# Sixteen on-chip transposes per attention head moved from TensorE to VectorE block turns with a trip through memory, with small edits at the start and the end

## The chip, the cores and the metric

One NeuronCore of one Trainium2 chip runs the whole program; nothing is shared with other cores. The metric is the device time of one execution in microseconds (us). TensorE (PE in the profile) does matrix products and transposes into PSUM, VectorE (DVE) and ScalarE (ACT) do elementwise work, GpSimd (POOL) does some more of it and issues a few DMAs, and SyncE (SP) issues nearly all DMAs, in order.

## The reference, cut to what matters

A two-layer decoder trunk on 1024 positions of width 1024, all in float32: first a gated linear recurrence (RG-LRU), then forgetting attention with 16 heads of 64, and a final RMS norm. The change is mostly in the attention:

```python
logits = einsum("bqhd,bkhd->bhqk", q_blk, kf) * scale
logits = logits + (cq_blk[..., :, None] - ck[:, :, None, :])   # cum: running sum of log sigmoid(f)
logits = where(kpos[None, :] <= qpos[:, None], logits, NEG_INF)
p = softmax(logits, axis=-1)
o = einsum("bhqk,bkhd->bqhd", p, vf)          # then y = o * silu(gate); y @ w_out
```

The mask is causal. The 1024 queries are 8 blocks of 128 rows, i = 0 to 7, and the keys 8 blocks of 128, j = 0 to 7; block i needs keys up to block i.

## The kernel before, in words

Every product is done in three float32r matmuls, high times high, high times low and low times high, so each operand is split into a high part (a cast, `to_hi`, mostly on ACT) and a low part (a subtraction, `to_lo`, mostly on DVE or POOL). Layer 0 takes the first 460 us or so of the span. Layer 1 then goes through 16 heads, two to a pair; while a head's attention runs, PE also computes the projections of the next pair (`kq_units`, `g_units`, `values`), which are called the fill here. One step of fill is six matmuls of 512 columns.

For one head hd there are four generators, and two calls of `run` interleave them by a string: a digit takes the next step of that generator, a dot takes one step of fill.

- `maxima(hd, c)` (L698) works on query blocks i = 4c to 4c+3. For each block PE computes the logits S (a PSUM tile of tag "S" with 1024 columns), DVE applies the mask and takes the row maximum in place (L715, "mask" below), and ACT writes the exponentials p to SBUF with their row sums (L720). These p have a query on each partition.
- `weigh(hd, c)` (L751) needs p with a key on each partition. For a pair of key blocks, PE transposes 128x128 pieces of p into a PSUM tile `pt`, also of tag "S" (L58); ACT and DVE split it into ph and pl (L85, L96); one step later PE adds V times ph and V times pl to the output O. The half c = 0 has the key pairs (0,1) and (2,3); the half c = 1 has (0,1), (2,3), (4,5) and (6,7). For c = 1 the pairs (0,1) and (2,3) are full: eight transposes each.

The first `run` of a head has `weigh(hd, 0)` as 0 and `maxima(hd, 1)` as 1, the second has `weigh(hd, 1)` as 0 and `maxima(hd + 1, 0)` as 1. The order strings are

```python
ORDER = "1.0.1.1.1.0.0", "10.1.0.1.01.0.0"              # heads 0 to 11
LAST = "1..0.1..1..1.0.0", "10..1.0..1.01..0..0"        # heads 12 to 15
```

PSUM tag "S" has two buffers, so a new S or pt has to wait until the last but one has been read by everybody. The instruction order of each engine within these rules is fixed when the program is built, by a planner that estimates times. Each engine then runs its own list strictly in order and waits on semaphores. SP's list too is in order: an issue that waits holds back all issues behind it. It holds the weight loads (`wf`), the loads of each head's K and Q parts (T, U; `load` and `load_q`) and the stores of finished heads (`y1d`).

At the start, SP loads a first piece of weights, then x in 16 pieces of 128x512 with the rest of the first weights in between; ACT squares each piece and makes its high part, DVE sums squares and makes the low part (`split_x`, `square_x`). At the end, `turned` makes the last rows, `root_mean` their norm, and SP stores them.

Of the kernel before, what the change touches and what calls it, by code (L numbers as in the profile page):

```python
# [11 lines left out]
F32 = mybir.dt.float32  # L12
# [26 lines left out]
def trunk(ctx: ExitStack, tc: tile.TileContext, xt, w0, wg, wo0, pc, gn, gf, w1, wv, wf, bf, wo1, out):  # L39
# [26 lines left out]
    epst = const.tile([P, 1], F32, name="epst")  # L66
    nc.vector.memset(epst, EPS)
    root = const.tile([P, 1], F32, name="root")
    nc.scalar.activation(root, epst, AF.Sqrt)
# [6 lines left out]
    pct = const.tile([P, 8, NB], F32, name="pct")  # L76
    gnt = const.tile([P, 2, KT], F32, name="gnt")
    cw = [pct[:, j] for j in range(4)]
# [26 lines left out]

    def split_weights(src, shape, hi_eng, lo_eng, parts=wpool):
        wt = loaded(shape)
        for part, sl in src:
            nc.sync.dma_start(wt[:, :, sl], part)
# [73 lines left out]
    with ExitStack() as l0:  # L183
# [41 lines left out]
        first = ([], [])  # L225
        early = [weights(w0[0], lo_eng=nc.vector), weights(w0[NB], lo_eng=nc.gpsimd)]
        k = 0
        for step in "uxnxgxuxgxxpxxxxxxxxxx":
            if step == "n":
                nc.sync.dma_start(gnt, gn)  # L230
            elif step == "p":
# [10 lines left out]
        def split_x(h, layer=0):  # L242
            for k, (hi, lo) in enumerate((raw, hT)[layer][h]):
                g_ = gnt[:, layer, k : k + 1]
                x = xs[h][k]
                to_hi(hi, x, nc.scalar, scale=g_)
                nc.vector.scalar_tensor_tensor(lo, x, g_, f32(hi), ALU.mult, ALU.subtract)
                yield
# [4 lines left out]
        def square_x(h):  # L253
            to = acc[:, halves[h]]
            sums[h].append(to)
            for k in range(KT):
                z = sq[k % 4] if k else to
                nc.scalar.activation(z, xs[h][k], AF.Square)
                if k == KT - 1:
                    sums[h].append(z)  # L260
                elif k:
                    nc.vector.tensor_tensor(to, to, z, ALU.add)
                yield
# [12 lines left out]

        for _ in zip(split_x(0), square_x(0)):
            pass

# [110 lines left out]
        for n in range(NB):  # L390
# [8 lines left out]
            if n == 0:  # L399
                gps = held[0] = two_banks("gps")  # L400
                product(gps[:, 0], 0, first[1])
                for _ in zip(split_x(1), square_x(1)):
                    pass
                done = norm_row(0)
            else:
# [86 lines left out]
    with ExitStack() as l1:  # L492
# [139 lines left out]
        def forget(half):  # L632
            cs = slice(half * HALF, (half + 1) * HALF)
            pt = ps.tile([P, HALF], F32, tag="O", name="fps")
            for i in range(4):
                if half and i > 1:
                    yield
                with tc.issue_after(pe[0].ins):
                    transpose(pt[:HEADS, i * P : (i + 1) * P], fz[:, half * 4 + i], ident)
            z_, e_ = (at.tile([HEADS, HALF], F32, tag=t, name=n, bufs=3) for t, n in (("ph", "z"), ("pl", "e")))  # L640
            parts = [at.tile([HEADS, HALF], F32R, tag=f"p{i + 2 * half}", name="cp", bufs=1) for i in (3, 4)]
            hi, lo = parts
# [47 lines left out]
        stats, ps_ = {}, {}  # L690

        def maxima(hd, c):

            s = hd % 2
            pair = hd // 2
            if c == 0:
                stats[hd] = at.tile([P, 8], F32, tag="sums", name="sums")
            sums = stats[hd]  # L698
            for i in range(4 * c, 4 * c + 4):
                n = (i + 1) * P  # L700

# [16 lines left out]

                p = ps_[i] = at.tile([P, n], F32, tag=f"p{i}", name="p", bufs=1)
                seen[0] = nc.scalar.activation(  # L720
                    p, S[:, :n], AF.Exp, bias=m, scale=-1.0, accum_out=sums[:, i : i + 1]
                )
# [26 lines left out]
        def weigh(hd, c, sub=slice(0, HALF)):  # L749
# [7 lines left out]
            O = ps.tile([P, HALF], F32, tag="O", name="O")[:, : end - begin]  # L757
            nj = end // P
            def products(j0, qlo, parts):
                for j, q, (ph, pl) in zip((j0, j0 + 1), qlo, parts):  # L760
                    v = V[j][:, 2 * s : 2 * s + 2].rearrange("p a d -> p (a d)")
                    o = O[:, q - begin :]
                    matmul(o, v, ph, start=j == 0, stop=False)
                    matmul(o, v, pl, start=False, stop=j == nj - 1)

            held = None
            for j0 in range(0, nj, 2):
                A = ps.tile([P, 2, HALF], F32, tag="S", name="pt")
                qlo = [max(begin, j * P) for j in (j0, j0 + 1)]
                ns = [end - q for q in qlo]  # L770
                for jj in range(2):
                    ks = slice((j0 + jj) * P, (j0 + jj + 1) * P)
                    for q in range(qlo[jj], end, P):
                        o = q - qlo[jj]
                        transpose(A[:, jj, o : o + P], ps_[q // P][:, ks], ident)
                parts = []
                for jj in range(2):
                    a = A[:, jj, : ns[jj]]
                    ph, pl = (at.tile([P, HALF], F32R, tag=t, name=t, bufs=3)[:, : ns[jj]] for t in ("ph", "pl"))
                    to_hi(ph, a, nc.scalar)  # L780
                    parts.append((ph, pl))
                for jj, (ph, pl) in enumerate(parts):
                    to_lo(pl, A[:, jj, : ns[jj]], ph, nc.vector)
                if held:
# [113 lines left out]
        def turned(c, q):  # L898
# [7 lines left out]
            elif q == 0:  # L906
                res = [tu.tile([P, SEQ], F32, tag=t, name="res") for t in ("U", "U0")]
            else:
                res = [tu.tile([P, SEQ], F32, tag="U1", name="res"), at.tile([P, SEQ], F32, tag="p7", name="res", bufs=1)]
            for b in range(2):  # L910
# [4 lines left out]
                for h, (d0, nd) in enumerate(parts):  # L915
# [6 lines left out]
                    for k in range(2):  # L922
# [5 lines left out]
                        if k == 0:  # L928
                            yield
                    sq = at.tile([P, HALF], F32, tag="xp", name="sq1", bufs=2)[:, : nd * P]  # L930
                    nc.scalar.activation(sq, pt, AF.Square, accum_out=ss[:, min(h, ss.shape[1] - 1)].unsqueeze(1))
# [6 lines left out]
                if c == 1:  # L938
# [3 lines left out]
                    nc.vector.tensor_scalar(res[b][:, hi], res[b][:, hi], r, None, ALU.mult)  # L942
# [6 lines left out]
        def root_mean(ss, between=lambda: None):  # L949

            ss = ss.rearrange("p (b h) -> p b h", h=2)
            r = ss[:, :, 0]
            nc.vector.tensor_tensor(r, r, ss[:, :, 1], ALU.add)
            between()
# [4 lines left out]
        late_w = []  # L959

        def late():
# [27 lines left out]
        load_q(1, 0)  # L989
        drain(fill)  # L990
        for hd in range(HEADS):
            pair = hd // 2
# [20 lines left out]
            first, second = LAST if hd > 11 else ORDER  # L1013
            run(first, weigh(hd, 0), maxima(hd, 1), fill=fill)
            if hd == HEADS - 1:
                break
            if hd == 14:
# [3 lines left out]
            gated(hd, 0)  # L1021
            side = late() if hd == 14 else iter(())
            if hd % 4 == 3 and hd < 12:
# [3 lines left out]
            run(second, weigh(hd, 1), maxima(hd + 1, 0), fill=fill, side=side)  # L1027
            drain(side)
            gated(hd, 1)
# [93 lines left out]
```

## Time and profile before

| | us |
|---|---|
| three runs | 1123.72, 1123.76, 1128.38 (median 1123.76) |
| the profiled execution | 1129.44 |
| its span | 1127.7 |
| PE busy in the span | 1114.3 (99%) |
| DVE, ACT, POOL busy | 758.6 (67%), 589.3 (52%), 195.6 (17%) |

The span is the time between the first and the last instruction of the profiled execution; 1.7 us lie around it. Starts in a timeline count from the span's start. Matmuls are pipelined: the duration in a row is that of one from its start to its modelled end, so what one costs PE is the distance between the starts of neighbours.

### The profile page before, as it was taken

The numbers are of one execution on the slowest core, as the hardware profiler recorded it, in microseconds if no ns is written. First come the engines' busy times: TensorE is split into PE (matmuls) and PEld (weight loads), VectorE is DVE, ScalarE is ACT, GpSimd is POOL, SyncE is SP. The second block draws the span as 40 slices with busy tenths as digits, with TensorE's granted clock in tenths as the row PEclk, the third lists the DMA queues.
The fourth block names the chain that finished last, engine by engine and source line by source line (L and its number), as shares of the span: only waits on it lengthen the run. The fifth ranks groups of instructions, "written<-read, shape, count | busy, mean of one in ns | idle before, by whom it ended". The sixth has DMA issues, their size and how long they took to land.

```text
span 1127.7 us, 15774 instructions
## 1 busy us (share of the span) xinstructions
PE 1114.3 (99%) x5691; PEld 936.8 (83%) x5691; DVE 758.6 (67%) x1268; ACT 589.3 (52%) x1081; POOL 195.6 (17%) x155
## 2 busy tenths in 40 slices
PE   9999999999999999999999999999999999999997
PEld 7788888888888887988888988889888898888786
DVE  7888755776568789656676466664667646676545
ACT  8488345355453656365555355553555535644335
POOL 1322112221121201431021110212102110021220
PEclk9999999999999999999999999999999999999999
DMA  6111111111111114433425224242252422564345
GB/s 235 57 47 42 51 52 52 38 58 45 52 38 52 47 44 145 129 112 102 112 71 123 66 77 117 72 118 71 74 119 73 118 71 77 176 189 158 117 154 187
DMA packets 62902, 105.43 MB, mean 93 GB/s; under 512 B 9796, under 2 KB 24772, under 8 KB 62824
## 3 DMA queue, kind: packets, MB, share of 16 engines
q1 hardware_dynamic: 59704, 95.97, 28.9%
q0 software_dynamic: 3120, 8.46, 2.3%
q8 instruction: 45, 0.74, 0.3%
q14 instruction: 33, 0.27, 0.1%
HBM read 63.30 MB, written 15.93 MB: 70 GB/s over the span
## 4 chain that ended last, share of the span: by engine, by line
PE 92%; DMA 2%; DVE 2%; issue 1%; ACT 1%; SPq 1%; POOL 0%; DVEq 0%; POOLq 0%; ACTq 0%
PE gps L54 33%; PE ops L54 16%; PE ups L54 12%; PE vps L54 8%; PE S L54 6%; PE O L54 6%; PE pt L58 5%; PE gate L54 3%; PE turn L54 3%; DMA wf<-in_wo 1%; DMA x<-in_xt 1%; POOL wl L96 0%; PE rsrow L54 0%; DMA wf<-in_w 0%; DMA yhl<-y1d 0%
## 5 line engine op out<-in xcount | busy, mean ns | idle before, releaser
L54 PE MATMUL gps<-hh,wh 128*128 128x512 f32 x576 | 229.1, 398 | 0.6 <-DVE qkl L595 0.6
L54 PE MATMUL gps<-hh,wl 128*128 128x512 f32 x576 | 226.8, 394 | 0.0
L54 PE MATMUL gps<-hl,wh 128*128 128x512 f32 x576 | 226.7, 394 | 0.0
L85 ACT CAST wh<-wf 128x512 fp32r<-128x512 f32 (+2 forms) x156 | 94.2, 607 | 147.8 <-PE ops L54 55.3
L96 POOL TENSOR_TENSOR wl<-wf,wh 128x512 fp32r<-128x512 f32 (+1 forms) x60 | 101.0, 1689 | 389.8 <-ACT wh L85 362.5
L720 ACT ACTIVATE p<-S,m 128x128 f32<-128x128 f32 (+7 forms) x128 | 94.8, 741 | 137.9 <-DVE m L715 136.8
L96 DVE TENSOR_TENSOR pl<-pt,ph 128x512 fp32r<-128x512 f32 (+1 forms) x198 | 98.7, 540 | 88.1 <-ACT ph L85 87.6
L54 PEld LDWEIGHTS gps<-hl,wh 128*128 128x128 f32 x576 | 108.3, 188 | 24.7 <-issue 0.5
L54 PEld LDWEIGHTS gps<-hh,wh 128*128 128x128 f32 x576 | 108.6, 189 | 20.5 <-DVE qkl L595 0.8
L54 PEld LDWEIGHTS gps<-hh,wl 128*128 128x128 f32 x576 | 108.7, 189 | 20.1 <-POOL wl L96 0.6
L715 DVE CUSTOM_DVE_ANT_0 S<-S,mask 128x128 f32<-128x128 f32 (+7 forms) x128 | 97.3, 761 | 28.8 <-PE S L54 28.8
L85 ACT CAST ph<-pt 128x512 fp32r<-128x512 f32 (+1 forms) x198 | 83.6, 473 | 36.2 <-PE pt L58 28.9
L54 PE MATMUL S<-T,U 96*128 96x512 f32 (+7 forms) x384 | 91.9, 348 | 2.7 <-ACT p L720 2.7
L96 DVE TENSOR_TENSOR wl<-wf,wh 128x512 fp32r<-128x512 f32 x96 | 70.7, 741 | 28.3 <-ACT wh L85 27.4
L381 DVE TENSOR_TENSOR x<-x,ops 128x512 f32<-128x512 f32 x80 | 54.1, 683 | 48.0 <-PE ops L54 48.0
L54 PEld LDWEIGHTS S<-T,U 128*128 128x128 f32 (+1 forms) x384 | 68.6, 190 | 16.1 <-ACT p L720 3.5
L58 PE MATMUL pt<-ident,p 128*128 128x128 f32 x576 | 79.4, 273 | 0.8 <-DVE pl L96 0.5
L58 PEld LDWEIGHTS pt<-ident,p 128*128 128x128 f32 x576 | 67.2, 140 | 13.9 <-issue 2.9
L54 PE MATMUL ups<-hh,wh 128*128 128x512 f32 x192 | 76.1, 397 | 1.1 <-ACT hh L87 1.1
L54 PE MATMUL ups<-hl,wh 128*128 128x512 f32 x192 | 76.7, 399 | 0.2
L54 PE MATMUL ops<-yh,wh 128*128 128x512 f32 x192 | 76.0, 396 | 0.5 <-DVE x L474 0.5
L54 PE MATMUL ups<-hh,wl 128*128 128x512 f32 x192 | 76.2, 397 | 0.0
(183 smaller groups left out, 2247.8 us busy)
## 6 DMA issues: line engine op xcount, KB each, us to landing
wf<-in_w SPq DMA_DIRECT2D x100, 256.0 KB
wf<-in_wo SPq DMA_DIRECT2D x64, 128.0 KB
U<-qkh SPq DMA_DIRECT2D x64, 128.0 KB
T<-qkh SPq DMA_DIRECT2D x28, 256.0 KB
x<-in_xt SPq DMA_DIRECT2D x16, 256.0 KB
x1d<-x SPq DMA_DIRECT2D x16, 256.0 KB
wf<-in_wv SPq DMA_DIRECT2D x16, 256.0 KB
U<-qkl SPq DMA_DIRECT2D x32, 128.0 KB
```

Of the source, the lines that this page charges most:

```text
L54: pe[0] = nc.tensor.matmul(*args, **kw)
L58: pe[0] = nc.tensor.transpose(*args)
L85: nc.scalar.copy(hi, src)
L96: return eng.tensor_tensor(lo, src, f32(hi), ALU.subtract)
L381: nc.vector.tensor_tensor(x, x, pt, ALU.add)
L715: nc.vector.tensor_tensor_reduce(S[:, :n], S[:, :n], mask[:, SEQ - n :], -1.0, -NEG, ALU.add, ALU.min, accum_out=m)
L720: seen[0] = nc.scalar.activation(p, S[:, :n], AF.Exp, bias=m, scale=-1.0, accum_out=sums[:, i : i + 1])
```

## The change

- **Scores of rows 512 to 1023.** In `maxima(hd, 1)` the exponential is taken in two ACT instructions: that of the first 512 keys goes back into S in PSUM, that of the others to p in SBUF as before. A new `turn_blocks` has DVE turn the first 512 columns of S in 32x32 blocks into an SBUF tile t32 (two buffers), which SP stores to a DRAM tile `turn` (256 KB, rows of 512 bytes); after each second block four SP loads (128 KB each, rows of 1 KB) bring it back into a tile PT with other partitions, so that a key stands on each. For a head that is four turns, four stores and eight loads. `turn_blocks` of block i-1 is called ahead of the logits of block i.
- **Products of rows 512 to 1023.** `weigh(hd, 1)` takes the key pairs in the order (4,5), (6,7), (0,1), (2,3). For the last two, ph and pl are made from PT and PE transposes nothing: 16 transposes of 128x128 for each head fewer.
- **Logits of block 0** are computed for 128 columns and no longer for 256.
- **Start:** the first piece of weights and the norm's gains are loaded from ACT's queue, x comes first on SP's queue, the first weights' high part is made on DVE, and squares of the first half of x are summed beside the second half. All eight squares are added before the norm's matmul.
- **End:** one of the last two stores goes out from ACT's queue, the norm's small addition is tied to its place ahead of the last scaling, and the last pair's weights (`late`) are spread thinner over the fill. Some tiles change tags.

```diff
@@ maxima
+            if c:
+                turn = dram.tile([P, 4, 4, P], F32, tag="turn", name="turn", bufs=2)
+                pts[hd] = at.tile([P, 4, 4, P], F32, tag="PT", name="PT", bufs=1)
             for i in range(4 * c, 4 * c + 4):
+                if i > 4:
+                    turn_blocks(hd, i - 1, ps_[i - 1][1], turn)
...
-                    hi_ = max(hi_, lo_ + 256)
+                    hi_ = max(hi_, lo_ + P)
...
-                p = ps_[i] = at.tile([P, n], F32, tag=f"p{i}", name="p", bufs=1)
+                if c:
+                    nc.scalar.activation(
+                        S[:, :HALF], S[:, :HALF], AF.Exp, bias=m, scale=-1.0, accum_out=sums[:, 4 + i : 5 + i]
+                    )
+                k0 = c * HALF
+                p = at.tile([P, n - k0], F32, tag=f"p{i}", name="p", bufs=1)
+                ps_[i] = p, S
                 seen[0] = nc.scalar.activation(
-                    p, S[:, :n], AF.Exp, bias=m, scale=-1.0, accum_out=sums[:, i : i + 1]
+                    p, S[:, k0:n], AF.Exp, bias=m, scale=-1.0, accum_out=sums[:, i : i + 1]
                 )
                 yield
+            if c:
+                turn_blocks(hd, 7, ps_[7][1], turn)
+                nc.vector.tensor_tensor(sums[:, 4:8], sums[:, 4:8], sums[:, 8:12], ALU.add)
@@ new
+        def turn_blocks(hd, i, S, turn):
+            t = at.tile([P, 4, 4, 32], F32, tag="t32", name="t32", bufs=2)
+            nc.vector.transpose(
+                t.rearrange("p b j q -> p j b q"), S[:, :HALF].rearrange("p (j b q) -> p j b q", b=4, q=32)
+            )
+            i -= 4
+            nc.sync.dma_start(turn[:, :, i], t.rearrange("p b j q -> p b (j q)"))
+            if i % 2:
+                two = slice(i - 1, i + 1)
+                for b in range(4):
+                    rows = slice(32 * b, 32 * b + 32)
+                    src = turn.rearrange("(a k) b i r -> b k a i r", a=4)[b][:, :, two]
+                    nc.sync.dma_start(pts[hd][rows, :, two], src)
@@ weigh
-            for j0 in range(0, nj, 2):
-                A = ps.tile([P, 2, HALF], F32, tag="S", name="pt")
+            k0 = c * HALF
+            js = [*range(k0 // P, end // P), *range(k0 // P)]
+            for j0 in js[::2]:
...
+                if j0 * P < k0:
+                    turned_ = [
+                        pts[hd].rearrange("p a i (j q) -> p j i a q", q=32)[:, j, rows] for j in (j0, j0 + 1)
+                    ]
+                else:
+                    A = ps.tile([P, 2, HALF], F32, tag="S", name="pt")
...
@@ start
+    wt0 = wpool.tile([P, 4, P], F32, tag="wf", name="wf", bufs=3)
+    nc.scalar.dma_start(wt0, w0[0, :, :4])
+    nc.scalar.dma_start(gnt, gn)
...
-        for step in "uxnxgxuxgxxpxxxxxxxxxx":
+        for step in "xxgxuxgxxpxxxxxxxxxx":
@@ end
-                    for hs in halves:
-                        nc.sync.dma_start(out[4 + 2 * q + b, :, hs], res[b][:, hs])
+                    for eng, hs in zip((nc.scalar if q * b else nc.sync, nc.sync), halves):
+                        eng.dma_start(out[4 + 2 * q + b, :, hs], res[b][:, hs])
```

More of the change, by code (lines that the diff above doesn't have):

```diff
@@ L104, in loaded, with split_weights @@
         return wpool.tile([P, *shape], F32, tag="wf", name="wf", bufs=3)
[L106 to L109, printed above, removed]
+    def split_weights(src, shape, hi_eng, lo_eng, parts=wpool, wt=None):
+        if wt is None:
+            wt = loaded(shape)
+            for part, sl in src:
+                nc.sync.dma_start(wt[:, :, sl], part)
         hi = parts.tile([P, *shape], F32R, tag="wh", name="wh")
@@ L225, in trunk @@
         first = ([], [])
-        early = [weights(w0[0], lo_eng=nc.vector), weights(w0[NB], lo_eng=nc.gpsimd)]
+        first[0].extend(split_weights(None, (4, P), nc.vector, nc.vector, wt=wt0))
+        early = [weights(w0[0, :, 4:], lo_eng=nc.vector), weights(w0[NB], lo_eng=nc.gpsimd)]
         k = 0
-        for step in "uxnxgxuxgxxpxxxxxxxxxx":
-            if step == "n":
-                nc.sync.dma_start(gnt, gn)
-            elif step == "p":
+        for step in "xxgxuxgxxpxxxxxxxxxx":
+            if step == "p":
                 nc.sync.dma_start(pct, pc)
@@ L275, in norm_row @@
             return nc.vector.reciprocal(r_, r_)
-        for _ in zip(split_x(0), square_x(0)):
-            pass
+        drain(split_x(0))
         state = {}
@@ L639, in forget @@
                     transpose(pt[:HEADS, i * P : (i + 1) * P], fz[:, half * 4 + i], ident)
-            z_, e_ = (at.tile([HEADS, HALF], F32, tag=t, name=n, bufs=3) for t, n in (("ph", "z"), ("pl", "e")))
-            parts = [at.tile([HEADS, HALF], F32R, tag=f"p{i + 2 * half}", name="cp", bufs=1) for i in (3, 4)]
+            z_, e_ = (at.tile([HEADS, HALF], F32, tag="pl", name=n, bufs=3) for n in "ze")
+            tags = ("t32", 2) if half else ("ph", 3)
+            parts = [at.tile([HEADS, HALF], F32R, tag=tags[0], name="cp", bufs=tags[1]) for _ in range(2)]
             hi, lo = parts
@@ L762, in products @@
                     o = O[:, q - begin :]
[L763 to L764 removed]
+                    matmul(o, v, ph, start=j == js[0], stop=False)
+                    matmul(o, v, pl, start=False, stop=j == js[-1])
             held = None
[L767 to L768 removed]
+            for j0 in js[::2]:
                 qlo = [max(begin, j * P) for j in (j0, j0 + 1)]
                 ns = [end - q for q in qlo]
[L771 to L775, printed above, removed]
+                if j0 * P < k0:
+                    rows = slice((begin - k0) // P, (end - k0) // P)
+                    turned_ = [
+                        pts[hd].rearrange("p a i (j q) -> p j i a q", q=32)[:, j, rows] for j in (j0, j0 + 1)
+                    ]
+                    view = lambda z: z.rearrange("p (i a q) -> p i a q", a=4, q=32)
+                else:
+                    A = ps.tile([P, 2, HALF], F32, tag="S", name="pt")
+                    for jj in range(2):
+                        ks = slice((j0 + jj) * P - k0, (j0 + jj + 1) * P - k0)
+                        for q in range(qlo[jj], end, P):
+                            o = q - qlo[jj]
+                            transpose(A[:, jj, o : o + P], ps_[q // P][0][:, ks], ident)
+                    turned_ = [A[:, jj, : ns[jj]] for jj in range(2)]
+                    view = lambda z: z
                 parts = []
                 for jj in range(2):
[L778 removed]
                     ph, pl = (at.tile([P, HALF], F32R, tag=t, name=t, bufs=3)[:, : ns[jj]] for t in ("ph", "pl"))
[L780 removed]
+                    to_hi(view(ph), turned_[jj], nc.scalar)
                     parts.append((ph, pl))
[L782 to L783 removed]
+                for (ph, pl), a in zip(parts, turned_):
+                    to_lo(view(pl), a, view(ph), nc.vector)
                 if held:
@@ L908, in turned @@
             else:
-                res = [tu.tile([P, SEQ], F32, tag="U1", name="res"), at.tile([P, SEQ], F32, tag="p7", name="res", bufs=1)]
+                res = [tu.tile([P, SEQ], F32, tag="U1", name="res"), at.tile([P, 2, SEQ], F32, tag="PT", name="res", bufs=1)[:, 0]]
             for b in range(2):
@@ L952, in root_mean @@
             r = ss[:, :, 0]
-            nc.vector.tensor_tensor(r, r, ss[:, :, 1], ALU.add)
-            between()
+            add = nc.vector.tensor_tensor(r, r, ss[:, :, 1], ALU.add)
+            with tc.issue_after(add.ins):
+                between()
             nc.scalar.activation(r, r, AF.Sqrt, bias=epst, scale=1.0 / SEQ)
@@ L959, in trunk, with spread @@
         late_w = []
+        def spread(gen, n):
+            for _ in gen:
+                for _ in range(n):
+                    yield
         def late():
@@ L990, in trunk @@
         drain(fill)
+        side = iter(())
         for hd in range(HEADS):
@@ L1013, in trunk @@
             first, second = LAST if hd > 11 else ORDER
-            run(first, weigh(hd, 0), maxima(hd, 1), fill=fill)
+            run(first, weigh(hd, 0), maxima(hd, 1), fill=fill, side=side)
             if hd == HEADS - 1:
+                drain(side)
                 break
@@ L1021, in trunk @@
             gated(hd, 0)
-            side = late() if hd == 14 else iter(())
+            if hd == 14:
+                side = spread(late(), 3)
             if hd % 4 == 3 and hd < 12:
```

18 lines of the change are left out of this document (8 added, 10 removed).

## The prediction

> **What bounds the kernel now.** I read the page's busy times and chain first, then the busy time by stretches, then PE, DVE and ACT in order of time through one head, then the DMA issues.
>
> ```profile
> span 1127.7 us, 15774 instructions
> PE 1114.3 (99%) x5691; PEld 936.8 (83%) x5691; DVE 758.6 (67%) x1268; ACT 589.3 (52%) x1081; POOL 195.6 (17%) x155
> PE 92%; DMA 2%; DVE 2%; issue 1%; ACT 1%; SPq 1%; POOL 0%; DVEq 0%; POOLq 0%; ACTq 0%
> 500.00:980.00 480.00, 478.93 (x2734) 415.16 (x2733) 302.92 (x637) 243.80 (x553) 63.37 (x51) 1.00 0.35 95
> ```
>
> PE is busy for 1114.3 of 1127.7 us and holds 92% of the chain that ended last. In the last row, most of the attention, it misses 1.1 of 480 us, while DVE is busy for 63% and ACT for 51% at full granted clock (1.00). So work taken off PE there is worth its full price, as long as PE is not made to wait. That is the question here: before, PE's list waits for almost nothing.
>
> **What comes off PE.** In PE's order of time, around the two full key pairs of one head's second half:
>
> ```profile
> 808.91 0.46 PE L54 MATMUL S<-T,U 128*128 128x256 f32 x2
> 809.20 1.04 PE L58 MATMUL pt<-ident,p 128*128 128x128 f32 x8
> 810.00 0.47 PE L54 MATMUL gps<-hh,wh 128*128 128x512 f32 x1
> 810.31 0.39 PE L54 MATMUL gps<-hh,wl 128*128 128x512 f32 x1
> 810.54 0.39 PE L54 MATMUL gps<-hl,wh 128*128 128x512 f32 x1
> ...
> 812.87 0.40 PE L54 MATMUL gps<-hl,wh 128*128 128x512 f32 x1
> 813.22 1.06 PE L58 MATMUL pt<-ident,p 128*128 128x128 f32 x8
> 814.04 0.48 PE L54 MATMUL O<-ph,v 128*128 128x512 f32 x1
> 814.36 0.40 PE L54 MATMUL O<-pl,v 128*128 128x512 f32 x1
> ...
> 824.38 0.28 PE L54 MATMUL O<-pl,v 128*128 128x256 f32 x1
> 824.49 0.22 PE L54 MATMUL O<-ph,v 128*128 128x128 f32 x1
> 824.55 0.28 PE L54 MATMUL O<-pl,v 128*128 128x128 f32 x1
> ```
>
> A matmul of 512 columns starts 0.23 us after its neighbour (810.31 to 810.54). The first eight transposes take 0.80 (809.20 to 810.00), and the matmul behind them 0.31 where 0.23 is usual: 0.88. The second group lies between 813.10 (812.87 + 0.23) and 814.04, and delays its successor by 0.09: 1.03. These two groups are what the change removes, so 1.9 us for a head, **30.5 us** for sixteen. The Trainium skill, VectorE: DVE Perf Modes, section "The three transpose paths", gives 390 ns for a 128x128 transpose on TensorE (bf16), by which 256 of them would be worth 100 us, and its "Rules for kernel authors" advise TensorE for 128x128 where PSUM will do. The spacing here, 0.10 us, contradicts that size and decides.
>
> Block 0's two logit matmuls fall from 256 to 128 columns. Rows of 256 columns lie 0.11 apart and rows of 128 columns 0.06 (824.38, 824.49, 824.55), so 2 x 0.06 x 16 = **1.9 us**.
>
> At the start PE waits for the second piece of x:
>
> ```profile
> 5.47 0.79 PE L54 MATMUL ups<-hh,wh 128*128 128x512 f32 x1
> 7.80 0.50 PE L54 MATMUL ups<-hh,wh 128*128 128x512 f32 x1 [0.81 <-ACT hh L87]
> 9.62 0.50 PE L54 MATMUL ups<-hh,wh 128*128 128x512 f32 x1 [0.30 <-ACT hh L87]
> ```
>
> With x first on SP and the first weights on ACT's queue, 0.81 + 0.30 can go; two squares now stand ahead of the first high part in ACT's list, which can lose as much. I take 1.0 saved there and 0.5 at the end (one store issue from another queue), with 0 to 2 as bounds. In all **34 us** come off.
>
> **What is put in PE's way.** An S tile is now free only after DVE has turned it, and the turn waits for both exponentials. From the changed program's order of instructions: logits of block 5 wait for the turn of block 4, those of 7 for the turn of 5, the transposes of pair (2,3) of the first half for the turn of 6, those of pair (4,5) for the turn of 7. I go through them with the times of one even head, whose blocks 6 and 7 stand at 801.32 and 803.53; prices follow in the same fence:
>
> ```profile
> 801.32 0.99 PE L54 MATMUL S<-T,U 128*128 128x512 f32 x4
> 802.14 0.39 PE L54 MATMUL gps<-hh,wh 128*128 128x512 f32 x1
> 803.53 1.10 PE L54 MATMUL S<-T,U 128*128 128x512 f32 x4
> 804.47 0.40 PE L54 MATMUL gps<-hh,wh 128*128 128x512 f32 x1
> 802.34 1.10 DVE L715 CUSTOM_DVE_ANT_0 S<-S,mask 128x896 f32<-128x896 f32 x1 [1.18 <-PE S L54]
> 803.36 0.14 DVE L715 DVE_READ_ACCUMULATOR2_ANT m<- 128x1 f32 x1
> 803.74 0.70 DVE L515 TENSOR_TENSOR gps<-gps,rs 128x512 f32<-128x512 f32 x1 [0.24 <-PE gps L54]
> 804.78 1.23 DVE L715 CUSTOM_DVE_ANT_0 S<-S,mask 128x1024 f32<-128x1024 f32 x1 [0.34 <-PE S L54]
> L96 DVE TENSOR_TENSOR pl<-pt,ph 128x512 fp32r<-128x512 f32 x91 | 60.0, 687 | 62.1 <-ACT ph L85 62.0
> 1114.87 0.49 DVE L942 TENSOR_SCALAR res<-res,ssq 128x512 f32<-128x512 f32 x1
> L720 ACT ACTIVATE p<-S,m 128x512 f32<-128x512 f32 x16 | 11.0, 687 | 25.9 <-DVE m L715 25.8
> L720 ACT ACTIVATION_READ_ACCUMULATOR p<-S,m 128x1 f32 x128 | 24.7, 193 | 0.0
> 807.21 0.53 ACT L85 CAST ph<-pt 128x256 fp32r<-128x256 f32 x2
> ```
>
> No row shows a block turn. The nearest is a DVE pass over 512 columns out of PSUM, 0.69; from SBUF one took 0.49, and an upper bound is the mask over 1024 columns, 1.23. I take 0.65. An exponential of 512 costs ACT 0.78 (687 + 193 ns, less the overlap of some 0.1).
>
> *Block 7 behind the turn of 5.* DVE's list has mask(6) ahead of that turn in heads 0 to 12. Mask(6) ends at 803.50 (803.36 + 0.14), the turn at 804.15, block 7 starts near 804.2 instead of 803.53: 0.67 us in each of the twelve heads that have only one fill step (1.39, 802.14 to 803.53) between blocks, **8 us** (6 to 15 with the bounds of the turn). From head 12 on there are two fill steps, which hide it.
>
> *Pair (2,3) behind the turn of 6.* In even heads that turn stands ahead of mask(7) and is done at 805.7 (block 6's second exponential ends near 805.0); PE comes there at 806.55. In odd heads mask(7) and a weight split stand ahead: the turn starts near 806.75 and ends at 807.4, 0.9 late in six heads: **5.4 us** (0 to 8).
>
> *Pair (4,5) behind the turn of 7.* Even: mask(7) to 806.9, exponential to 807.7, the two casts ph (0.53) to 808.2, exponential to 809.0, turn to 809.65; PE arrives at 809.57. About 0.1 in six heads, **1 us** (0 to 4). Odd: the wait before has made room.
>
> *The way through memory.*
>
> ```profile
> x1d<-xp POOLq DMA_DIRECT2D x16, 256.0 KB, 3.4
> recd<-rc POOLq DMA_DIRECT2D x15, 4.0 KB, 2.5
> L654 SPq DMA_DIRECT2D cumd<-cp x4: 325/326/331, 487.8 to 504.8; - x4
> L607 SPq DMA_DIRECT2D T<-cumd x18: 243/253/927, 490.2 to 991.3; - x18
> L616 SPq DMA_DIRECT2D U<-qkh x32: 467/590/1550, 468.1 to 1008.7; - x32
> ```
>
> A store from SP and the load that depends on it were issued 2.4 us apart (487.8 to 490.2, 32 KB); POOL's stores took 2.5 for 4 KB and 3.4 for 256 KB. For the 256 KB store I take 2.6, nearest SP's own row. By the Trainium skill (DMA: Bandwidth & Descriptors, "Anatomy of one DMA") a DMA costs some 2.0 us and its bytes over 436 GB/s, 2.6 too, which the 3.4 row exceeds. Four loads are issued at 0.55 each, as U's are, and land 2.5 later. Even head: turned at 809.65, stored by 812.3, loads issued by 814.5, landed at 817.0, 12.8 after block 7's start at 804.2. Four casts and four subtractions follow; the lists of ACT and DVE have two masks and two exponentials of the next head among them, so that the last subtraction ends some 5.9 later, at 822.9. PE asks for the first of them after block 7 (its issue ends at 805.14) and seven fill steps (9.8), the transposes and products of three other pairs and the next head's four logit blocks (5.1 together), at 820.0, and for the last 3.0 later, at 823.0: 0.1 to spare. Odd head: SP's list has more in it. The next head but one's T loads wait there for block 7, then come the four loads of blocks 4 and 5, the store of 6, three U loads, and only then the store of 7 and three more issues ahead of the last four loads. In the same way I get PT 1 to 3 us later after block 7 than in an even head; PE itself, held up by 0.9 at pair (2,3), asks 0.9 later, so it waits for 0.1 to 2.1, and some more at the second cast: 0.5 to 2.6. I take 1.5 in six heads, **9 us** (3 to 16). While ACT and DVE stand before the missing PT, the next head's masks and exponentials queue behind them; that is why the last cast, not the first, is the late one. Heads 12 to 15 have more fill and less of this; with the last head, which has little left to do while it waits, I put **3 us** (1 to 7).
>
> ACT gains four exponentials with read-outs a head (some 0.45 each, since the row of 512 and that of the rest replace one longer row), DVE four turns; at 51% and 63% neither becomes the bound on its own. DMA moves 32 MB more at 0.35 busy.
>
> **Sum.** -34 + 8 + 5.4 + 1 + 9 + 3 = -7.6 us. The profiled execution took 1129.44 for its span of 1127.7; it would take about 1121.8. Against the median of the three runs, 1123.76, the same difference gives **1116 us**. The bounds: with the least of each cost -34 + 6 + 0 + 0 + 3 + 1 = -24, with the most -34 + 15 + 8 + 4 + 16 + 7 = +16.
>
> **Rivals.**
>
> *Everything is hidden*: the turns find DVE idle earlier than I think and PT is there in time; what is left of the waits is 3 us or so. DVE idles for 37% of the attention, which speaks for it; the turn of 5 standing behind mask(6) in the list speaks against. -34 + 3 = -31: 1093 us.
>
> *The round trip becomes the bound*: with SP's one list and T's 256 KB in the shared queues, store and load take 3.4 us each, as POOL's 256 KB store does, and not 2.6 and 2.5. Then PT is 1.7 later in every head. It decides from the 0.1 to spare in even heads: 1.6 there and 1.7 more in odd ones, (1.6 + 1.7) x 6 = 20, and some 3 in the last heads. -7.6 + 23 = +15: 1139 us, slower. For it: U issues of up to 1.55 us in the last row above; against: 0.35 mean DMA share.
>
> *The turn is dear*: at 1.2 us instead of 0.65 the three waits grow by 0.55 x (12 + 6 + 6) = 13 and PT comes 0.55 later, in six odd heads 3: -7.6 + 16 = +9, 1132 us. Only the bound row speaks for it.
>
> That the transposes stay on PE can be excluded: PE's list has 256 fewer. The gain at the start may be nothing; that is within the bounds.
>
> **How the numbers follow.** A difference below 0.5% (5.6 us) is about what a measurement of this kernel cannot tell from no change. Chances: my forecast 0.50 (its own range 1106 to 1124), everything hidden 0.20, the round trip 0.22, the dear turn 0.08. Faster by over 0.5% means below 1118.1: 0.31 of my forecast's 0.50 and all of the hidden case, 0.51. Within: 0.17 of the forecast and 0.03 of the others, 0.20. Slower: 0.29. The range 1095 to 1139 leaves out half of the hidden case and a third of the round trip.
>
> **What would show it.** Right: L58's matmuls 320 instead of 576; PE busy some 30 us less; new idle of PE ahead of S and pt released by DVE's turn, some 14 us in all, 0.7 at a time, and none from head 12 on; ACT waiting for DMA PT in odd heads; SP's longest waits on its own `turn` stores. A turn near 0.65 us in the groups. Wrong: PE idle that is released by ACT's ph from PT in every head (round trip), or no new PE idle at all (hidden), or idle of PE in layer 0 or ahead of weights (wl), which I have at nothing because weight loads are issued a head ahead.

## The result, and the profile after

| | before | after |
|---|---|---|
| median of six runs each, same chip (us) | 1125.57 | 1178.88 (1171.45 to 1181.14) |
| ratio, 95% interval | | 1.0466 (1.0443 to 1.049) |
| profiled execution, its span | 1129.44, 1127.7 | 1171.45, 1169.7 |

The change makes the kernel 4.7% slower. I had predicted 1116 us with a range of 1095 to 1139. The profiled execution is the fastest of the six after, which go from 1171.45 us at a mean granted clock of 0.984 to 1181.14 at 0.979, so the trace shows less of the loss than the medians; one execution of run 9 below, 2214.08 us, is left out of its ratio.

The page of the kernel after, its span and busy times:

```profile
span 1169.7 us, 15802 instructions
PE 1110.0 (95%) x5431; PEld 914.0 (78%) x5431; DVE 803.3 (69%) x1351; ACT 609.3 (52%) x1208; POOL 191.9 (16%) x155
```

The stretch of 500 to 980 us in the busy times by stretches, and then PE's longest waits (us in total, times, longest):

```profile
500.00:980.00 480.00, 445.89 (x2375) 371.43 (x2374) 314.24 (x656) 243.32 (x617) 59.49 (x48) 0.98 0.53 140
```
```profile
PE O L54 <- DVE pl L99: 15.9, 19, 2.9
PE O L54 <- ACT ph L88: 12.9, 12, 2.4
PE S L54 <- DVE t L700: 9.2, 15, 2.9
PE pt L58 <- DVE t L700: 3.9, 6, 0.7
```

PE now lacks 34.1 of those 480 us where it lacked 1.1. More than half of its waiting is 28.8 us ahead of the products O, for ph and pl. PE's granted clock is 0.98 over the stretch, and the DMA engines are busy for 0.53 instead of 0.35. The span grew by 42.0 us: PE idles 59.7 us instead of 13.4 (46.3 more), while its busy time fell by only 4.3.

One odd head (head 1) shows what happens. Rows of SP, ACT, DVE and PE in order of time:

```profile
558.43 0.56 SPq L704 DMA_DIRECT2D turn<-t  x1
559.04 0.64 SPq L616 DMA_DIRECT2D U<-qkh  x1
...
561.06 1.38 SPq L704 DMA_DIRECT2D turn<-t  x1
...
564.69 1.94 SPq L710 DMA_DIRECT2D PT<-turn  x4
...
571.57 0.62 ACT L88 CAST ph<-PT 128x512 fp32r<-128x512 f32 x1 [6.27 <-DMA U<-qkh]
572.22 2.15 DVE L99 TENSOR_TENSOR pl<-PT,ph 128x512 fp32r<-128x512 f32 x1 [6.18 <-DMA U<-qkl]
572.24 0.49 PE L54 MATMUL O<-ph,v 128*128 128x512 f32 x1 [1.84 <-ACT ph L88]
574.42 0.49 PE L54 MATMUL O<-pl,v 128*128 128x512 f32 x1 [1.69 <-DVE pl L99]
576.68 0.80 PE L54 MATMUL O<-ph,v 128*128 128x512 f32 x1 [1.77 <-ACT ph L88]
578.10 0.79 PE L54 MATMUL O<-pl,v 128*128 128x512 f32 x1 [0.63 <-DVE pl L99]
...
579.12 0.63 PE L54 MATMUL gps<-hh,wl 128*128 128x512 f32 x1
579.55 0.63 PE L54 MATMUL gps<-hl,wh 128*128 128x512 f32 x1
```

The turn of block 7 ended at 558.2, its store was issued at 561.06, the last four loads at 564.69, and ACT got PT at 571.57, after standing still for 6.27 us. (The releaser named is another DMA that landed near that time; among the semaphores that ACT waits for are those of the four loads, and the last landing that the trace has for them is at 571.47.) So the way took 2.8 us in SP's list, 3.6 from the store's issue to its landing, 1.9 to issue four loads, and 4.8 more until the last of them landed. Then everything for PE comes late in turn: four stops of 0.63 to 1.84 us. (The first subtraction took 2.15 us instead of 0.69; run 5 shows why.) Matmuls of 512 columns start 0.43 apart at 579.12, where 0.23 is usual. Stretches of 2 us, from busy PE to POOL, then the granted clock, the DMA share and GB/s:

```profile
568.00:570.00 2.00, 2.00 (x12) 1.71 (x11) 0.00 (x0) 0.00 (x0) 0.00 (x0) 1.00 0.99 220
570.00:572.00 2.00, 0.40 (x2) 0.00 (x0) 0.00 (x0) 0.43 (x1) 0.53 (x1) 1.00 1.02 251
572.00:574.00 2.00, 0.49 (x1) 0.19 (x1) 1.78 (x1) 0.18 (x1) 1.92 (x2) 1.00 0.61 148
574.00:576.00 2.00, 0.49 (x1) 0.19 (x1) 0.90 (x3) 1.07 (x3) 1.49 (x1) 0.88 0.00 0
576.00:578.00 2.00, 0.80 (x1) 0.29 (x1) 1.86 (x5) 1.61 (x4) 0.00 (x0) 0.50 0.05 9
578.00:580.00 2.00, 1.90 (x5) 1.51 (x6) 1.34 (x3) 0.82 (x3) 0.00 (x0) 0.50 0.73 243
```

While PT is awaited all DMA engines are busy (0.99, 1.02). After some 5 us in which PE does little (570.4 to 575.5), its clock is granted at 0.50 for 6.8 us. The same follows the stops of heads 5 and 9 (6.8 us each), and 3.4 us follow four times elsewhere: 34 us of half clock ahead of the end, of which PE is busy for 28, so that it loses some 14 to 17 us. The kernel before has two stretches of 3.4 us. One of them follows a single wait of 2.69 us, so its trace had shown this price:

```profile
1049.94 0.74 PE L54 MATMUL S<-T,U 128*128 128x512 f32 x2 [2.69 <-ACT p L720]
1052.00:1054.00 2.00, 2.00 (x6) 1.55 (x5) 1.63 (x5) 0.78 (x2) 0.27 (x1) 0.50 0.00 0
```

Summed from PE's order of time, the waits ahead of O are 5.9, 2.4, 4.6, 1.5, 4.7 and 1.4 us in the odd heads 1 to 11, but 0.2 to 1.0 in the even ones 0 to 10; 6.0 us follow in heads 12 to 15. PT was nearly as late in heads 3, 7 and 11 as in 5 and 9, but there matmuls of the values' projection stand between the waiting products.

### The profile page after: what moved, and what is told of

Same layout as the page of the kernel before. It is cut to its first block, busy times and chain, and to the rows that moved or that the text cites. A ratio compares the mean times of both kernels' runs of the same rounds, so it can differ in the third digit from the quotient of the medians.

```text
span 1169.7 us, 15802 instructions
## 1 busy us (share of the span) xinstructions
PE 1110.0 (95%) x5431; PEld 914.0 (78%) x5431; DVE 803.3 (69%) x1351; ACT 609.3 (52%) x1208; POOL 191.9 (16%) x155
## 5 line engine op out<-in xcount | busy, mean ns | idle before, releaser
L54 PE MATMUL gps<-hh,wh 128*128 128x512 f32 x576 | 231.7, 403 | 0.7 <-DVE qkl L596 0.7
L54 PE MATMUL gps<-hl,wh 128*128 128x512 f32 x576 | 229.1, 398 | 0.0
L99 POOL TENSOR_TENSOR wl<-wf,wh 128x512 fp32r<-128x512 f32 (+1 forms) x60 | 98.0, 1641 | 393.8 <-ACT wh L88 370.0
L54 PEld LDWEIGHTS gps<-hh,wh 128*128 128x128 f32 x576 | 109.9, 191 | 20.5 <-DVE qkl L596 0.9
L54 PE MATMUL S<-T,U 96*128 96x512 f32 (+9 forms) x384 | 93.4, 352 | 10.5 <-DVE t L700 9.2
L752 ACT ACTIVATE p<-S,m 128x128 f32<-128x128 f32 (+3 forms) x128 | 67.8, 530 | 64.2 <-DVE m L740 62.2
L99 DVE TENSOR_TENSOR pl<-PT,ph 128x512 fp32r<-128x512 f32 (+1 forms) x68 | 51.0, 772 | 62.6 <-ACT ph L88 44.1
L54 PE MATMUL O<-pl,v 128*128 128x512 f32 (+1 forms) x198 | 68.8, 366 | 15.9 <-DVE pl L99 15.9
L99 DVE TENSOR_TENSOR wl<-wf,wh 128x512 fp32r<-128x512 f32 x96 | 67.9, 710 | 22.2 <-ACT wh L88 22.1
L54 PE MATMUL O<-ph,v 128*128 128x512 f32 (+1 forms) x198 | 70.5, 364 | 12.9 <-ACT ph L88 12.9
L746 ACT ACTIVATE S<-S,m 128x512 f32<-128x512 f32 x64 | 42.3, 661 | 71.6 <-DVE m L740 71.5
```

The source lines that it names most:

```text
L54: pe[0] = nc.tensor.matmul(*args, **kw)
L99: return eng.tensor_tensor(lo, src, f32(hi), ALU.subtract)
L746: nc.scalar.activation(S[:, :HALF], S[:, :HALF], AF.Exp, bias=m, scale=-1.0, accum_out=sums[:, 4 + i : 5 + i])
L752: seen[0] = nc.scalar.activation(p, S[:, k0:n], AF.Exp, bias=m, scale=-1.0, accum_out=sums[:, i : i + 1])
```

## The experiments

Each run is compared with runs of the kernel before on the same chip; ratios are to those. Differences to the kernel after are of medians; by the ratios they are 1 to 2 us smaller.

**1. The change without the turn.** `maxima` and `weigh` as before (with 128 columns for block 0), and the tiles that go with them.

```diff
-            if c: turn_blocks(...); js = (4,5),(6,7),(0,1),(2,3); ph, pl from PT
+            p[:, :n] in one exponential; js = (0,1) ... (6,7); pt by PE transposes
```

> The change without the turn: the edits at the start and the end and the 128 columns for block 0 stay; the scores of rows 512 to 1023 are one exponential and sixteen transposes a head again. All theories put the loss into the turn and what hangs on it, so this should take 1120 to 1126 us beside 1125 us before. Above 1135 us, the small edits would carry part of the loss.

1127.82 us against 1124.21, ratio 1.003 (1.0019 to 1.0042), a little above the 1120 to 1126 expected. So nearly all of the loss hangs on the turn, but the small edits, which I had put at 1.9 + 1 + 0.5 saved, cost 3.6.

**2. No trip.** PT is one constant tile, without store and loads.

```diff
-            nc.sync.dma_start(turn[:, :, i], ...); nc.sync.dma_start(pts[hd][rows, :, two], src)
+            # neither; pts[hd] = still, a tile set to zero once
```

> The turns stay on VectorE, the store and the loads go; ph and pl of the last two key pairs are made from one constant tile, so two of the four key pairs are left out of the sum. Theory (the trip through memory is late, PE idles before it, and the granted clock halves behind the idle time): PE's waits ahead of O fall from some 27 us to under 3, the halved clock goes, 1105 to 1118 us. Rival (the split exponentials, the turns and the longer hold of the logits' buffers cost most): 1150 us or more, with the waits still there.

1128.79 us, ratio 1.0032 (1.0019 to 1.0046): 50 us less than the kernel after, so the trip is the main cause. But it is 11 us above the top of what I expected, and no better than without any turn. PE's waits for pl stay at 5.4 us. DVE, with POOL's rows behind it:

```profile
854.78 4.56 DVE L99 TENSOR_TENSOR pl<-PT,ph 128x512 fp32r<-128x512 f32 x3
853.95 2.55 POOL L775 TENSOR_TENSOR sg<-sg,recb 64x1024 f32<-64x1024 f32 x1 [2.97 <-DMA recb<-recd]
856.58 1.62 POOL L839 TENSOR_TENSOR yo<-yo,sg 128x512 f32<-128x512 f32 x1
```

Three subtractions that take 1.9 us elsewhere (0.69 each, 0.6 apart) take 4.56 beside POOL's two products.

**3. The turn in even heads only** (0 to 10), with the small edits; in the other heads ACT writes the first 512 scores to the PT tile and PE transposes from there.

```diff
+        def by_turn(hd): return hd % 2 == 0 and hd < 12
```

> The turn only in heads 0, 2, 4, 6, 8 and 10, whose PT came nearly in time; the other ten heads transpose on PE again (their first 512 scores go to the PT tile by ACT, in two exponentials as before). Theory: each of the six gains 1.9 us and pays some 0.9, so with the 2 to 4 us of the small edits 1115 to 1123 us, no halved clock. Rival (the trip is too long in every head, and even heads only looked better because odd ones had set them back): waits ahead of O of 1 us or more in even heads and over 1127 us.

1125.74 us, ratio 1.0006 (0.9995 to 1.0018): above the 1115 to 1123 expected, because I had still counted the small edits as a gain. Against run 1 the six turns bring 2.1 us, the clock isn't halved in the attention, and waits ahead of O are 1.3 us in all. But the 2.1 us needn't be the turn's own gain: run 1 has six waits of 0.2 us ahead of S for p, which are gone here, and run 8 bears on that.

**4. T and U loads of the next head but one behind PT's in SP's list.**

```diff
-                load(hd + 2, ...)
+                with tc.issue_after(back[hd].ins):      # the last PT load of head hd
+                    load(hd + 2, ...)
```

> As the changed kernel, but the T and U loads of the next head but one stand behind the last PT loads in SP's list, in all heads. Theory (PT is late in odd heads because these 1.5 MB stand ahead of it in SP's list and fill the DMA engines, whose busy share was 0.9 to 1.0 there): PE's waits ahead of O fall from some 27 us to under 10, most of the halved clock goes, 1130 to 1150 us. Rival (the trip itself, store then load, is too long): the same waits, 1170 to 1182 us.

1156.69 us, ratio 1.0286 (1.026 to 1.0313): 22 us better, but 22.7 us of waits ahead of O are left, neither the "under 10" of the one nor the "same" of the other. Over 500 to 980 PE is busy for 447.65 us, after it was 445.89: the gain is mostly in heads 12 to 15. In heads 1 to 11 the run doesn't settle whether the order in SP's list is to blame, since the edit leaves three other U loads (of `load_q`) ahead of the store. Head 1 of this run:

```profile
559.44 0.59 SPq L616 DMA_DIRECT2D U<-qkh  x1
...
561.41 0.86 SPq L704 DMA_DIRECT2D turn<-t  x1
565.83 1.74 SPq L710 DMA_DIRECT2D PT<-turn  x4
```

The turn of block 7 ended at 559.4, so its store still stood 2.0 us in the list, and the PT loads were issued no earlier than in the kernel after (564.69). In the odd heads 1 to 11 the store was issued 2.0 to 3.8 us after the turn, against 2.8 to 3.5 in the kernel after.

**5. As 2, and POOL's products left out** (the gate times the reciprocal row sums, sg times recb, and the output times that, yo times sg).

> As the kernel without the trip, and GpSimd's products (sg times recb, yo times sg, about 4 us a head) are left out. There three subtractions pl<-PT took 4.56 us at 854.78 while GpSimd was at work, 0.69 each elsewhere. Theory (a subtraction whose operands all lie in SBUF stands still while GpSimd works, one out of PSUM doesn't; this is a price of reading PT from SBUF): every pl<-PT falls to 0.7 us, PE's 5.4 us of waits ahead of O for pl go, and the halved clock at 575 with them: 1117 to 1123 us beside 1128.8. Rival (these subtractions are late because masks and weight splits stand ahead in VectorE's list): waits of 4 us or more stay, 1126 to 1131 us.

1118.23 us, ratio 0.9942 (0.9919 to 0.9965): 10.6 us less than run 2. No wait of PE ahead of O is left among the longest. The groups of run 2 and then of this run (busy, mean ns):

```profile
L99 DVE TENSOR_TENSOR pl<-PT,ph 128x512 fp32r<-128x512 f32 (+1 forms) x68 | 62.9, 948 | 6.6 <-ACT ph L88 6.5
```
```profile
L99 DVE TENSOR_TENSOR pl<-PT,ph 128x512 fp32r<-128x512 f32 (+1 forms) x68 | 43.4, 655 | 9.1 <-ACT ph L88 9.0
```

So it is POOL that stretches the subtraction. The trace of before had already shown this, and that a subtraction out of PSUM is not stretched:

```profile
565.49 2.19 DVE L96 TENSOR_TENSOR wl<-wf,wh 128x512 fp32r<-128x512 f32 x1 [1.42 <-ACT wh L85]
567.61 1.14 DVE L96 TENSOR_TENSOR pl<-pt,ph 128x512 fp32r<-128x512 f32 x2
564.75 2.39 POOL L747 TENSOR_TENSOR sg<-sg,recb 64x1024 f32<-64x1024 f32 x1 [4.28 <-DMA recb<-recd]
567.21 1.61 POOL L802 TENSOR_TENSOR yo<-yo,sg 128x512 f32<-128x512 f32 x1
```

There wl, with both inputs in SBUF, took 2.19 us until POOL's product was over (567.14), and pl, with one input in PSUM, ran at 0.57 each beside POOL's next one. The Trainium skill, SBUF — State Buffer, section "Who interferes with whom", states this rule: a DVE instruction with two SBUF inputs contends with a GpSimd instruction that reads SBUF, over shared ports that are an exclusive lock, and one with at most one SBUF input (outside the two-port modes) does not. The traces agree: wl ended 0.54 us after POOL's product did. What the kernel before would gain without POOL's products was not run; all stops of its PE come to 7.0 us.

**6. No T and U loads from head 2 on.**

```diff
         def load(hd, ...):
+            if hd > 1: return                           # the same in load_q
```

> The changed kernel with the loads of T and U left out from head 2 on (their place in SP's list and their bytes; heads 2 to 15 use the first two heads' T and U). The turn's store and loads stay as they are. Theory (the trip is late in odd heads because those loads stand ahead of it in SP's list and share the DMA engines): PE's waits ahead of O, 28.8 us, fall under 10, 1130 to 1145 us, no more than 3.4 us of halved clock from 500 us on. Rival (store, semaphore and loads are too slow on their own): over 20 us of these waits stay, 1165 us or more.

1150.11 us, ratio 1.0224 (1.0203 to 1.0246): 29 us less than the kernel after, and 5 above the range expected. Median times from issue to landing (us, last column) of the kernel after, then of this run, and PE's waits in this run:

```profile
turn<-t SPq DMA_DIRECT2D x64, 256.0 KB, 2.8
PT<-turn SPq DMA_DIRECT2D x128, 128.0 KB, 3.1
T<-qkh SPq DMA_DIRECT2D x28, 256.0 KB, 5.4
```
```profile
PT<-turn SPq DMA_DIRECT2D x128, 128.0 KB, 2.8
```
```profile
PE O L54 <- DVE pl L99: 17.6, 17, 3.2
PE O L54 <- ACT ph L88: 1.4, 4, 0.5
```

Waits for ph, which come straight from a late PT, fall from 12.9 to 1.4 us: the loads were what made PT late. By the trace they do it mostly by their place: in the odd heads 1 to 11 the store of block 7 is now issued 0.1 to 1.2 us after the turn instead of 2.8 to 3.5, and the whole way takes 8.2 to 9.4 us instead of 10.8 to 13.2, while from the store's issue on it takes about as long as in the kernel after in heads 3 to 11 (7.3 to 9.3 us here, 7.7 to 9.0 there). A run with their bytes at another place was not made. The waits for pl do not fall (15.9 to 17.6), so the total missed "under 10", and 3.4 us of half clock stay three times. In head 5, POOL's products (718.90 to 722.94) stretch wl to 2.51 us and hold back the mask and three pl behind it, with PE stopped for 3.20 us until 723.54. That a PT coming early enough clears the subtractions from POOL's way in more heads (run 2) fits, but was not tried by itself.

**7. Work in PE's idle time.** 21 matmuls of zero weights before the waiting products in heads 1, 5 and 9.

```diff
+                    for _ in range(6): matmul(o, zeros, hT[0][0][0], start=False, stop=False)
                     matmul(o, v, ph, ...)               # and 6 or 3 ahead of pl
```

> The changed kernel with 21 matmuls of zero weights (4.9 us of PE's time) put ahead of the products that wait for PT in heads 1, 5 and 9, where PE idles 5.9, 4.6 and 4.7 us and the granted clock is halved for 6.8 us each time. They add nothing to the sums. Theory (the clock is halved because PE was idle, so that work in the idle time keeps it): no halved clock in the three heads; each saves 3.4 us less 0.5 for zeros that end late: 1168 to 1173 us, PE busy 15 us more. Rival (the clock follows something else, such as DMA or power): the halved stretches stay, 1178 us or more.

1166.38 us, ratio 1.037 (1.0348 to 1.0391), a little below the range expected: 12.5 us less than the kernel after by the medians (10.8 by the ratios), by adding 14.7 us of work to PE. In the profiled executions block 7's mask of head 11 comes 7.4 us earlier (918.33 instead of 925.77). Head 1 again:

```profile
572.00:574.00 2.00, 2.00 (x10) 1.63 (x9) 0.75 (x3) 1.53 (x4) 1.21 (x1) 1.00 1.01 270
...
576.00:578.00 2.00, 0.85 (x4) 0.48 (x3) 2.00 (x5) 1.28 (x3) 0.88 (x1) 1.00 0.46 162
578.00:580.00 2.00, 2.00 (x10) 1.60 (x10) 1.22 (x3) 0.59 (x1) 0.00 (x0) 1.00 0.27 104
```

The clock stays at 1.00 in all three heads, with the DMA engines as full as before. So the halving follows from PE's idleness. The Trainium skill, TensorE: Matmul & The Clock Gate, section "What's actually happening", says so: the clock is halved after at least one idle window of about 3.4 us. The traces agree in so far as the stretches of half clock last 3.4 or 6.8 us, and add that such a window need not be empty: in head 1 PE had a matmul about every 2 us, and in the kernel before a wait of 2.69 us was enough.

**8. The kernel before with the turn in the six even heads**, none of the small edits. 

> The kernel before with the turn in heads 0, 2, 4, 6, 8 and 10 alone, and none of the edits at the start, the end and block 0. The same turn gained 2.1 us beside the small edits alone (1125.7 against 1127.8). Theory (the small edits cost 3.5 us, the turn in even heads gains): 1120 to 1123 us, faster than before by 0.1 to 0.4%. Rival (the turn's gain in even heads only made up for a loss by the 128 columns of block 0): 1124 to 1126 us.

1124.0 us, ratio 0.9995 (0.9976 to 1.0014): not to be told from before, and in the range of the rival, not in the theory's 1120 to 1123. That fits a gain of run 3 over run 1 that mostly made up for the 128 columns of block 0. In the profiled run each of the six waits for the turn ahead of block 7 (2.6 us in all) is there.

**9. As 8, with one fill step moved ahead of block 7.**

```diff
+TURN = "1.0.1.1..1.0.0", "10.1.01.01.0.0"              # heads with the turn
```

> As the kernel before with the turn in six even heads, and in these heads one step of fill is moved: two of them stand between the logits of blocks 6 and 7, and none between the last key pairs' first step and the next head's block 2. Theory (block 7 starts 0.60 us late in each of the six because the turn of block 5 stands behind the mask of 6 in VectorE's list): the six waits of 0.42 us ahead of S for t go, 3 to 4 us less than the 1124.0 there, 1119 to 1122 us, faster than before by 0.2 to 0.5%. Rival (the step is missed where it is taken from, block 2 then waits for the buffer of block 1): 1123 us or more, with new waits ahead of S for p.

1121.6 us, ratio 0.9973 (0.9955 to 0.999), faster than both kernels, by 0.27%. Of the waits for t one of 0.2 us is left in PE's list, and no wait for p took their place:

```profile
PE O L55 <- DVE pl L97: 1.6, 5, 0.4
PE S L55 <- DVE pl L97: 1.2, 1, 1.2
```

**10 and 11. Block 0's 128 columns alone; the start alone.** 

> The kernel before with 128 columns instead of 256 for block 0, nothing else. The prediction: 1.9 us less. Theory from the small edits alone, where the time from one block 7 to the same a pair of heads on was 59.4 and 82.4 us against 59.1 and 82.1 before: 1 to 3 us more. In both, within 0.3% of before.

 

> The kernel before with the edits at the start alone. The prediction: 1 us less, 0 to 2. Theory from the small edits alone, where PE's first product of layer 0 started at 6.52 us instead of 5.47, the clock stayed halved until 10.5 us, and a wait of 1.56 us ahead of a gate appeared at 104: 1 to 2.5 us more.

1126.76 us, ratio 1.0015 (0.9998 to 1.0031), and 1127.36 us, ratio 1.0026 (1.0009 to 1.0044). Block 0's two matmuls and their successor, before (256 columns) and in run 10 (128), there with the next block's:

```profile
525.89 0.46 PE L54 MATMUL S<-T,U 128*128 128x256 f32 x2
526.18 1.04 PE L58 MATMUL pt<-ident,p 128*128 128x128 f32 x8
```
```profile
525.85 0.39 PE L54 MATMUL S<-T,U 128*128 128x128 f32 x2
526.08 1.06 PE L58 MATMUL pt<-ident,p 128*128 128x128 f32 x8
...
528.72 0.50 PE L54 MATMUL S<-T,U 128*128 128x256 f32 x2 [0.20 <-ACT p L720]
```

The two matmuls take 0.29 us with 256 columns and 0.23 with 128: 0.06 saved, half of the price that I had put on it, and about 1 us in sixteen heads. Against it, in six heads block 1 waits 0.20 us for p and starts 0.36 late, 2.2 us in all. The interval of run 10 touches 1, so that the edit costs anything is not shown; that it gains nothing like 1.9 is. Run 11 lost more than the 1 to 2.5 us expected. At the start (run 1, whose start edits are those of the kernel after):

```profile
6.52 0.80 PE L54 MATMUL ups<-hh,wh 128*128 128x512 f32 x1 [0.82 <-ACT hh L249]
104.22 0.50 PE L54 MATMUL gate<-xch,wgh 128*128 128x512 f32 x1 [1.56 <-ACT th L314]
```

The first product starts at 6.52 instead of 5.47, the matmuls stay 0.43 apart until 10.5, and a stop of 1.56 us appears ahead of a gate. The late start and the stop come with the start edits (run 11 has both); the spacing of 0.43 need not, since in run 11 and in the kernel after the matmuls are mostly 0.23 apart from 7.8 us on. Why ACT has th later I have not followed.

## Why the prediction was wrong, point by point

- **Transposes, 1.9 us a head: right.** L58's matmuls are 320 instead of 576. With trip and POOL out of the way (run 5), block 7's mask of head 6 starts 57.7 us after that of head 4, against 59.4 in run 1. That is 1.7 less for two heads in spite of stops worth 2 x 0.60 + 0.84, so 3.7 gross. The 100 us that the prediction worked out from the 390 ns of the Trainium skill (VectorE: DVE Perf Modes, "The three transpose paths") do not fit this.
- **Block 7 behind the turn of 5: right (0.60, predicted 0.67).** After, block 7 of head 2 starts at 591.75 with 0.43 idle; its predecessor started at 590.92, so it is 0.60 late. A stop costs some 0.17 more than its idle time, since the matmul ahead of it is seen to its end. PE has 68 stops instead of 11; these and the half clock, which stretches its matmuls, are why busy time fell by 4.3 us and not by 30.
- **Pair (2,3) behind the turn of 6: right (0.63 to 0.68 idle in six odd heads, 3.9 us in all, 5.4 predicted). Pair (4,5): nothing, 1 predicted.** The turn itself took 0.715 us, 0.65 predicted.
- **"None from head 12 on": wrong.** PE waits 2.89 and 0.98 us for t in head 13 (1017.89 and 1027.77). There DVE's list has the subtractions of stored rows (yhl) ahead of the turns, which I had not looked for.
- **The trip, 9 + 3: the step that failed.** I gave store, issue and loads 7.35 us, and let PT be late by 0.5 to 2.6 in odd heads. In the even heads 0 to 10 the trace has 7.7 to 8.7 us from the turn's end to the last landing, so that price was near. In the odd heads 1 to 11 it has 10.8 to 13.2: I had seen that SP's list puts T and U loads in between, but PT landed there 15.8 to 18.2 us after block 7's start against 13.2 to 14.2 in even heads, where I had added 1 to 3; in head 1 the engines were full besides (0.99 to 1.02 DMA share), where I had argued from a mean of 0.35. PE's waits ahead of O came to 20.5 us in the odd heads 1 to 11, 6.0 from head 12 on and 2.4 in the even ones, where I had 9, 3 and 0. And the sum had nothing for what such waits set off, the halved clock. Without the T and U loads 29 us go (run 6), without the trip 50 (run 2). Of the 42.4 us between the profiled executions of the kernel after and of run 2, 22.6 are waits ahead of O, up to 14 are half clock (27 us less of it), and 4 come from 25 fewer stops.
- **The round-trip rival (0.22) had the right wait and the wrong size.** It put the slow hops alike in all heads and priced only the wait. In the trace the even heads wait 0.2 to 1.0 us, and what neither sum has is the halved clock that a wait sets off (10.8 to 12.5 us from three heads in run 7).
- **Casting and subtracting from PT was costed as from pt: wrong.** Subtractions with both inputs in SBUF wait for POOL: 10.6 us in run 5.
- **Small edits, 3.4 saved: wrong, 3.6 lost.** I priced block 0 by neighbours of another kind (products of O 0.06 apart), where its pair saved 0.06 instead of 0.12 and block 1 came to wait for p, and gave the start a gain from an issue order without following ACT's list behind it.

The sum: predicted -7.6, measured +53.3 by the medians. The trip gave 50 instead of 12, POOL 10.6 instead of 0, the small edits +3.6 instead of -3.4: together 56 of the 61 between the two. The waits of head 13 (3.9) and the one of 1.2 in head 0 make up the rest as near as can be told.

## What to carry to other kernels

Price a round trip from the list of the queue that issues it: whose issues stand between the producer's end and the store, and between the store's landing and the loads. Take the DMA share of the 10 us in which it runs, not the mean. An operand moved from PSUM to SBUF changes who its reader collides with: look in the old trace for an instruction with the same operand homes beside the same neighbour. A stop of PE that recurs within a few microseconds can cost its length and then the clock; work put into the gap, even useless work, can be cheaper than the gap.

## What the runs showed of the hardware that I had not expected

- A DVE subtraction of 128x512 out of SBUF takes 0.69 us alone and up to 2.84 beside a POOL product; out of PSUM it keeps its time.
- PE's clock fell to 0.50 for 6.8 us after some 5 us with a matmul every 2 us, and for 3.4 us after a single wait of 2.69 us; it didn't fall where zero matmuls filled the gaps.
- Two logit matmuls in the same place take PE 0.23 us with 128 columns and 0.29 with 256.
- A block turn of 128x512 float32 out of PSUM takes DVE 0.715 us.
